# Two blocks of conditioning products moved ahead of the sums of squares, with their landing places, before the first MLP

## The chip, the cores and the metric

The kernel runs on one core of one Trainium2 chip. The metric is the device time of one execution in microseconds (us); several executions are taken and their median is quoted. TensorE (PE in the profile) multiplies, VectorE (DVE) and ScalarE (ACT) work on tiles element by element, GpSimd (POOL) does a few small things, SyncE (SP) issues the DMA transfers. Each engine has its own instruction stream, works it off in order, and waits on semaphores for the others.

## The reference

Two layers over 512 latent and 256 context tokens of width 1024. What matters here is layer 0: a pooling mixer, a gated residual, a root-mean-square norm with a shift and a scale that come from a conditioning vector, and a squared-ReLU MLP.

```
sh1, sc1, g1, sh2, sc2, g2 = split(silu(c) @ ada_w[i] + ada_b[i], 6)     # six vectors of 1024
h = h + g1 * pool_mix(modulate(rms_norm(h, norm_g[i, 0]), sh1, sc1))
m = rms_norm(h, norm_g[i, 1]) * (1 + sc2) + sh2
h = h + g2 * (square(relu(m @ mlp_w1[i])) @ mlp_w2[i])
```

The same is done for the context tokens with a second conditioning vector. The product `silu(c) @ ada_w[0]` has 6144 columns and is cut into twelve blocks of 512: blocks 6 and 7 are the shift `sh2`, blocks 8 and 9 the scale `sc2`, blocks 10 and 11 the second gate.

## The kernel before

Activations lie with the 1024 features on the partitions, as eight tiles of 128 features (`KT` = 8); a tile has 512 latent columns (`h_lat`) and 256 context columns (`h_ctx`).

A block b of the conditioning is made in two steps. `ada0_products(b)` loads four pieces of 512 KB (`adaw[0, b, u]`) and multiplies them on TensorE, eight matmuls of 512 columns that use 32 columns of the array each (L192; a matmul shows as two records); ACT then copies the sums to a row (L195). `ada0_done(b)` transposes that row on TensorE (L201), DVE sums it and adds the bias (L204, L206), and for some blocks makes the factor `am` (L160). Below, P6 is the products of block 6, T6 its transposes, and so on.

Where the pieces land differs by block. Most go into a ring of seven buffers (`praw`), two pieces into a ring called `mc`, blocks 6 and 8 into two large tiles, `m_hi` and `m_lo`, that held the turned inputs of the mixer until its last pooling matmul and will hold the MLP's input afterwards. Block 4 had landed in two buffers of the ring `w`, in which the weights are split into a high and a low part (`load_w`: ACT copies, L91; DVE subtracts, L92).

The loop over `dt` makes the eight output tiles of the mixer (L668); DVE adds each to `h` (L353), ACT squares it, and POOL adds the squares into one tile for latent and one for context (L272, `accs`). The last tile's squares are left in tiles of their own (`tails`, L680). Then come, in this order on TensorE: P6, the sums of squares over the partitions (matmuls against a column of ones, 24 records, L287), T6, P8, the spreading of the reciprocal roots over the partitions (12 records, L302; the roots are made by DVE at L289 and POOL at L291), T8, P9, and the first MLP matmuls.

The MLP's input is made in twelve units, in the order latent, latent, context of two feature tiles each. For unit u, `normed(u)` multiplies on DVE (L737 latent, L735 context), `moved(u)` makes the high part on ACT (L748; for context L745 twice and L746), `used(u)` makes the low part on DVE (L759, L757) and issues the unit's six latent or twelve context matmuls (L764) against the first two weight tiles (`ws`). The loop runs normed(u), moved(u-1), used(u-2); it is written out by hand, and so is the order on TensorE from the mixer on, and on DVE and ACT from the sums of squares to the units' end. Elsewhere a scheduler places instructions. TensorE's products of block 10 (P10) are placed by it between the units.

Of the kernel before, what the change touches and what calls it, by code (L numbers as in the profile page):

```python
# [8 lines left out]
F32 = mybir.dt.float32  # L9
F32R = mybir.dt.float32r  # L10
AF = mybir.ActivationFunctionType
# [3 lines left out]
P = 128  # L15
D = 1024
KT = D // P
# [30 lines left out]
def dit_block_kernel(ctx: ExitStack, tc: tile.TileContext, xT, cols, adab, adaw, w1, w2, wqkv, wo,  # L48
                     poolw, gvec, rope, edge, eye, out):
    nc = tc.nc  # L50
    act, dve, pool, pe = nc.scalar, nc.vector, nc.gpsimd, nc.tensor
# [5 lines left out]
    big = sb(ctx, "big", 1)  # L57
    wp = sb(ctx, "wp", 4)
    rp = sb(ctx, "rp", 2)
    sc = sb(ctx, "sc", 4)  # L60
# [14 lines left out]
    def new(p, shape, dt, tag, bufs=None):  # L75
        uid[0] += 1
        kw = {"bufs": bufs} if bufs else {}
        return p.tile(shape, dt, tag=tag, name=f"{tag}{uid[0]}", **kw)
# [8 lines left out]
    def ps_aux():  # L87
        return new(aux, [P, 512], F32, "aux")
# [21 lines left out]
    landing = {}  # L110
# [35 lines left out]
    def load_w(src, lo_eng=dve, ring=None, raw=None):  # L146

        t = new(wp, [P, 2, 1024], F32R, "w")
        if raw is None:
            raw = new(*(ring or (raws, [P, 1024], F32, "raw")))  # L150
            nc.sync.dma_start(raw, src)
        hilo(t[:, 0], t[:, 1], raw, lo_eng)
        return t
# [19 lines left out]
    def ada0_products(b):  # L173

        ps = ps_aux()
        for u in range(4):
            if (b, u) in ((5, 3), (9, 3)):

                t = new(mc, [P, 1024], F32, "mc")
                nc.sync.dma_start(t, adaw[0, b, u])  # L180
            elif b in landing:
                t = landing[b][:, u]
                nc.sync.dma_start(t, adaw[0, b, u])
            elif early:
                t = early.pop(0)
            else:
                t = new(*praw)
                nc.sync.dma_start(t, adaw[0, b, u])
            for kk in range(2):
                kt = 2 * u + kk  # L190
                o = kt % CG * (P // CG)
                pe.matmul(ps[o : o + P // CG, :512], s_w[:, kt], t[:, kk * 512 : kk * 512 + 512],  # L192
                          start=kt < CG, stop=kt >= KT - CG)
        row = new(sc, [P, 512], F32, "sc")
        act.activation(row, ps[:, :512], AF.Copy)  # L195
        return row
# [48 lines left out]
    def hs(k0, k1, c0, n):  # L245

        if c0 < SEQ:
            return h_lat[:, k0:k1, c0 : c0 + n]
        return h_ctx[:, k0:k1, c0 - SEQ : c0 - SEQ + n]
# [14 lines left out]
    def squares(acc, k, w, c0, n, place=None, eng=dve):  # L264

        if acc is None:
            acc = new(accp[0], [P, w, n], F32, accp[1]) if place is None else place
            act.activation(acc, hs(k, k + w, c0, n), AF.Square)
        else:
            sq = new(sc, [P, w, n], F32, "sc")  # L270
            act.activation(sq, hs(k, k + w, c0, n), AF.Square)
            eng.tensor_tensor(acc, acc, sq, op=ALU.add)  # L272
        return acc
# [386 lines left out]
    accs = [None, None]  # L660
# [7 lines left out]
                pe.matmul(ps[:, c0 : c0 + w], lhs, pooled[dt // 2][:, kc, ax, c0 : c0 + w], start=n == 0, stop=n == 5)  # L668
        return ps

    tails = []

    def mixed(dt, ps):
        for s, c0, n in segs:
            add_gated(dt, ps[:, c0 : c0 + n], gp, c0, n)
            if dt < KT - 1:
                accs[s] = squares(accs[s], dt, 1, c0, n, eng=pool)
            else:
                tails.append(new(sc, [P, 1, n], F32, "sc"))
                act.activation(tails[s], hs(dt, dt + 1, c0, n), AF.Square)  # L680

    row = ada0_products(2)
    tile0 = pool_tile(0)
# [8 lines left out]
    for dt in range(8):  # L692
        ps = mix(dt)
        if dt in (0, 3):
            row = ada0_products(3 + 2 * (dt > 0))
        elif dt == 4:
            ada0_done(5, row)
        mixed(dt, ps)
        if dt == 1:
            ada0_done(3, row)  # L700
        if dt in (1, 2, 3, 4):
            scaled(*pool_tile(dt + 3))

        if dt == 4:
            for b, tag in ((6, "m_hi"), (8, "m_lo")):
                landing[b] = big.tile([P, 4, D], F32, tag=tag, name=f"block{b}")
            ws = [load_w(w1[0, t]) for t in range(2)]
        if dt == 5:
            row = ada0_products(7)
        elif dt == 6:  # L710
            ada0_done(7, row)
    row = ada0_products(6)

    by_hand.enter_context(tc.manual_schedule(engines={mybir.EngineType.DVE, mybir.EngineType.Activation}))
    stats = ps_aux()
    rrs = [rstd_cols(n, [accs[s], tails[s]], stats[:, 4 * s : 4 * s + n // P]) for s, _, n in segs]
    ada0_done(6, row)
    row = ada0_products(8)  # L720
    rbs = [spread(rrs[s], n, ps_aux()[:, :n]) for s, _, n in segs]
    ada0_done(8, row)
    m = new_m("m")

    units = [u for k in range(0, KT, 2) for u in ((0, k, 1), (0, k + 1, 1), (1, k, 2))]
# [41 lines left out]
    for u in range(len(units) + 2):  # L767
        if u < len(units):
            normed(u)
        if 0 < u <= len(units):  # L770
            moved(u - 1)
        if u > 1:
            used(u - 2)

        if u == 1:
            last = ada0_products(9)
        elif u == 3:
            ada0_done(9, last)
    ws = [load_w(w1[0, 2 + t]) for t in range(2)]
    by_hand.close()  # L780
# [439 lines left out]
```

## Time and profile before

| | |
|---|---|
| three runs, median | 1252.46 us (1251.32 to 1253.43) |
| the profiled execution, its own time | 1251.34 us |
| its span, first to last instruction | 1249.2 us |
| mean granted TensorE clock | 0.996 of 2.4 GHz |
| TensorE busy | 1222.6 us, 98% |
| DVE, ACT, POOL busy | 1016.9, 589.5, 143.1 us |

The stretch that the change touches runs from about 25 us (where block 4's buffers come free) to about 96 us (the end of the units). The profile gives each engine's instructions with a start and a duration, and in brackets the idle time before it with what ended it; the granted clock is 1.00 at 2.4 GHz and 0.50 at 1.2 GHz.

### The profile page before, as it was taken

How to read it: one execution, taken by the hardware profiler on the slowest of the kernel's cores; microseconds unless marked ns; L12 is line 12 of the kernel's file. 1: busy time of each engine (PE TensorE's matmuls, PEld its weight loads, DVE VectorE, ACT ScalarE, POOL GpSimd, SP SyncE). 2: the span in 40 equal slices, each digit the busy share in tenths (PEclk: the TensorE clock that was granted, in tenths of full speed). 3: DMA queues.
4: the chain of work that ended last, by engine and by line, in shares of the span. 5: the costliest groups of instructions: out<-in, count | busy, mean ns of one | idle time of the engine just before them, and what ended most of it. 6: DMA issues, size and time to landing. Idle time of an engine off the chain costs nothing.

```text
span 1249.2 us, 20001 instructions
## 1 busy us (share of the span) xinstructions
PE 1222.6 (98%) x7896; PEld 1080.2 (86%) x7896; DVE 1016.9 (81%) x1723; ACT 589.5 (47%) x1055; POOL 143.1 (11%) x129
## 2 busy tenths in 40 slices
PE   7999999999999999999999999999999999999996
PEld 4767888899999999999988888888988999999996
DVE  6564998888989788866888387879899989898986
ACT  6554533444444444334455264554565454545443
POOL 0300000122131322231012001000000000000002
PEclk9999999999999999999999999999999999999998
DMA  9866424333433333321122020211223332323201
GB/s 351 329 238 218 136 85 139 114 119 119 153 111 133 129 123 120 129 68 34 46 82 85 17 85 18 68 34 67 102 86 101 111 109 92 111 94 110 75 28 68
DMA packets 41310, 138.64 MB, mean 111 GB/s; under 512 B 4736, under 2 KB 8064, under 8 KB 41088
## 3 DMA queue, kind: packets, MB, share of 16 engines
q1 hardware_dynamic: 41216, 137.36, 32.0%
q8 instruction: 62, 1.02, 0.3%
q14 instruction: 32, 0.26, 0.1%
HBM read 135.25 MB, written 2.10 MB: 110 GB/s over the span
## 4 chain that ended last, share of the span: by engine, by line
PE 63%; issue 27%; DVE 4%; ACT 2%; DMA 2%; POOL 1%; SPq 0%; POOLq 0%; DVEq 0%; ACTq 0%
PE aux L495 10%; PE mm L495 10%; PE aux L889 7%; PE mm L444 5%; PE aux L464 5%; PE mm L376 5%; PE aux L444 4%; PE aux L1009 3%; PE aux L998 3%; PE mm L967 2%; DMA raw<-in_dram 2%; PE aux L192 1%; PE mm L668 1%; PE mm L764 1%; PE aux L988 1%
## 5 line engine op out<-in xcount | busy, mean ns | idle before, releaser
L495 PE MATMUL aux<-act,w 128*128 128x512 f32 (+1 forms) x1224 | 238.8, 346 | 0.3 <-DVE h_lat L353 0.2
L495 PE MATMUL mm<-act,w 128*128 128x512 f32 (+1 forms) x1224 | 237.2, 345 | 0.9 <-DVE h_lat L353 0.9
L495 PEld LDWEIGHTS mm<-act,w 128*128 128x128 f32 x1224 | 194.9, 189 | 31.6 <-DVE h_lat L353 1.1
L495 PEld LDWEIGHTS aux<-act,w 128*128 128x128 f32 x1224 | 194.7, 189 | 29.6 <-DVE h_lat L353 0.7
L92 DVE TENSOR_TENSOR w<-raw,w 128x1024 fp32r<-128x1024 f32 x106 | 129.3, 1224 | 28.4 <-ACT w L91 28.3
L91 ACT ACTIVATE w<-raw 128x1024 fp32r<-128x1024 f32 x106 | 110.2, 1056 | 77.6 <-PE aux L495 40.7
L353 DVE SCALAR_TENSOR_TENSOR h_lat<-aux,mod,h_lat 128x512 f32<-128x512 f32 (+1 forms) x180 | 122.4, 686 | 16.9 <-PE aux L495 14.2
L433 POOL TENSOR_TENSOR sc<-pair 128x512 f32<-128x512 f32 x55 | 80.0, 1462 | 314.2 <-DMA raw<-in_dram 106.7
L353 DVE SCALAR_TENSOR_TENSOR h_lat<-mm,mod,h_lat 128x512 f32<-128x512 f32 (+1 forms) x140 | 97.7, 700 | 5.5 <-PE mm L495 4.6
L376 PE MATMUL mm<-m_m_hi,w 128*128 128x512 f32 (+1 forms) x320 | 92.9, 352 | 0.2 <-ACT m_m_hi L91 0.2
L889 PE MATMUL aux<-w,a_m_hi 128*128 128x256 f32 (+1 forms) x384 | 86.3, 320 | 0.0
L224 DVE SCALAR_TENSOR_TENSOR mc<-raw,s_f,mc 128x512 f32<-128x512 f32 x112 | 83.7, 765 | 2.1 <-DMA raw<-in_dram 1.3
L444 PE MATMUL mm<-m_m_hi,mc 128*128 128x256 f32 x384 | 69.8, 281 | 0.0
L889 PEld LDWEIGHTS aux<-w,a_m_hi 128*128 128x128 f32 x384 | 63.4, 190 | 5.0
L376 PEld LDWEIGHTS mm<-m_m_hi,w 128*128 128x128 f32 x320 | 56.3, 189 | 10.2 <-ACT r L384 0.8
L464 PE MATMUL aux<-m_c,w 128*128 128x256 f32 x528 | 61.6, 276 | 0.0
L889 PE MATMUL aux<-w,a_m_lo 128*128 128x256 f32 (+1 forms) x192 | 61.2, 319 | 0.0
L464 PEld LDWEIGHTS aux<-m_c,w 128*128 128x128 f32 x528 | 60.8, 188 | 0.0
L444 PEld LDWEIGHTS mm<-m_m_hi,mc 128*128 128x128 f32 x384 | 59.4, 188 | 0.5
L291 POOL TENSOR_TENSOR sm<-sm,neghalf 128x2 f32<-128x2 f32 (+1 forms) x9 | 6.6, 738 | 443.4 <-DVE sm L289 443.4
L376 PE MATMUL mm<-m_m_lo,w 128*128 128x512 f32 (+1 forms) x160 | 56.1, 351 | 0.7 <-DVE m_m_lo L92 0.7
L444 PE MATMUL mm<-m_m_lo,mc 128*128 128x256 f32 x192 | 53.9, 281 | 0.0
(260 smaller groups left out, 2453.9 us busy)
## 6 DMA issues: line engine op xcount, KB each, us to landing
raw<-in_dram SPq DMA_DIRECT2D x155, 512.0 KB, 3.8
praw<-in_dram SPq DMA_DIRECT2D x34, 512.0 KB, 7.7
fin<-in_dram SPq DMA_DIRECT2D x24, 512.0 KB, 4.4
pair<-in_dram SPq DMA_DIRECT2D x22, 512.0 KB, 4.6
block<-in_dram SPq DMA_DIRECT2D x8, 512.0 KB, 7.2
h_lat<-in_dram SPq DMA_DIRECT2D x4, 512.0 KB, 6.3
w<-in_dram SPq DMA_DIRECT2D x4, 512.0 KB, 10.7
out_dram<-fin SPq DMA_DIRECT2D x8, 256.0 KB, 2.5
```

Of the source, the lines that this page charges most:

```text
L91: act.activation(hi, src, AF.Copy)
L92: lo_eng.tensor_tensor(lo, src, hi.bitcast(F32), op=ALU.subtract)
L224: dve.scalar_tensor_tensor(acc[:, s], w, scal, acc[:, s], op0=ALU.mult, op1=ALU.add)
L353: dve.scalar_tensor_tensor(h, ps, gate[:, dt, s : s + 1], h, op0=ALU.mult, op1=ALU.add)
L376: pe.matmul(ps[:, c0 : c0 + cn], lhs, ms(m, ax, k, c0, cn), start=k + wx + ax == 0, stop=k == KT - 1 and wx == 1)
L433: eng.tensor_tensor(t, x, y, op=how)
L444: pe.matmul(places[n], w[:, wx, k * P : k * P + P], inputs[n][ax][:, k], start=k + wx + ax == 0, stop=k == 3 and wx == 1)
L464: pe.matmul(pc[:, t * 256 : t * 256 + 256], ws[k // 4][:, wx, k % 4 * P : k % 4 * P + P], ms(m, ax, k, SEQ, CTX), start=k + wx + ax == 0, ...
L495: pe.matmul(ps, lhs, a[:, t, ax, c0 : c0 + n], start=t + wx + ax == 0, stop=t == 1 and wx == 1)
L889: pe.matmul(ps, lhs, ws[u][:, wx, o : o + width], start=k + ax + wx == 0, stop=k == KT - 1 and ax == 1)
L998: pe.matmul(po, v[:, vx, k, g * HD : g * HD + HD], pT[:, px, k, j0:j1].rearrange("p j q -> p (j q)"), start=k + vx + px == 0, stop=k == 5 ...
L1009: pe.matmul(ps, ws[j][:, wx, dt * P : dt * P + P], o[ax][:, j, c0 : c0 + n], start=j + wx + ax == 0, stop=j == 1 and ax == 1)
```

## The change

Block 7 lands in two buffers of the ring `w` (those that block 4 used); block 6 lands in the `praw` ring; only block 8 keeps a large tile, `m_hi`. The first two weight tiles `ws` are made behind the mixer's loop in the program instead of in its fifth step. P8 stands directly behind P6 and ahead of the sums of squares, T8 directly behind T6. The last tile's squares are added to `accs` by DVE, so that the sums of squares take one tile each and not two. P9 is issued at unit step 2 instead of 1, T9 at step 4 instead of 3.

```diff
         for u in range(4):
-            if (b, u) in ((5, 3), (9, 3)):
+            if b == 7:
+                if u % 2 == 0:
+                    pair = new(wp, [P, 2, 1024], F32, "w")
+                t = pair[:, u % 2]
+                nc.sync.dma_start(t, adaw[0, b, u])
+            elif (b, u) in ((5, 3), (9, 3)):
...
     def mixed(dt, ps):
         for s, c0, n in segs:
             add_gated(dt, ps[:, c0 : c0 + n], gp, c0, n)
-            if dt < KT - 1:
-                accs[s] = squares(accs[s], dt, 1, c0, n, eng=pool)
-            else:
-                tails.append(new(sc, [P, 1, n], F32, "sc"))
-                act.activation(tails[s], hs(dt, dt + 1, c0, n), AF.Square)
+            accs[s] = squares(accs[s], dt, 1, c0, n, eng=pool if dt < KT - 1 else dve)
...
         if dt == 4:
-            for b, tag in ((6, "m_hi"), (8, "m_lo")):
-                landing[b] = big.tile([P, 4, D], F32, tag=tag, name=f"block{b}")
-            ws = [load_w(w1[0, t]) for t in range(2)]
+            landing[8] = big.tile([P, 4, D], F32, tag="m_hi", name="block8")
...
-    row = ada0_products(6)
+    ws = [load_w(w1[0, t]) for t in range(2)]
+    rows = [ada0_products(6)]
...
+    rows.append(ada0_products(8))
     stats = ps_aux()
-    rrs = [rstd_cols(n, [accs[s], tails[s]], stats[:, 4 * s : 4 * s + n // P]) for s, _, n in segs]
-    ada0_done(6, row)
-    row = ada0_products(8)
+    rrs = [rstd_cols(n, [accs[s]], stats[:, 4 * s : 4 * s + n // P]) for s, _, n in segs]
+    ada0_done(6, rows[0])
+    ada0_done(8, rows[1])
     rbs = [spread(rrs[s], n, ps_aux()[:, :n]) for s, _, n in segs]
-    ada0_done(8, row)
...
-        if u == 1:
+        if u == 2:
             last = ada0_products(9)
-        elif u == 3:
+        elif u == 4:
             ada0_done(9, last)
```

TensorE, from the last product of block 6 to the first unit. `aux_` tiles are banks of PSUM, `sc_` the rows and squares, `mc_425` and `mc_428` the summed squares, `sm_` the roots. Before (line 192 is a product, 287 the sums of squares, 201 transposes, 302 the spreading, 764 a unit):

```order
L287 MATMUL aux_714<-ones,sc_695 128x1
L201 MATMUL aux_735<-ident,sc_710 128x128 x4
L192 MATMUL aux_743<-block_598,s_w_146 32x512 x8
L302 MATMUL aux_758<-ident,sm_725 128x128 x4
L302 MATMUL aux_763<-ident,sm_733 128x128 x2
L201 MATMUL aux_766<-ident,sc_756 128x128 x4
L192 MATMUL aux_788<-praw_789,s_w_146 32x512 x2
```

Of the change, the same place (198 a product, 293 the sums of squares, 207 transposes, 308 the spreading, 763 a unit):

```order
L198 MATMUL aux_717<-block_597,s_w_146 32x512 x8
L293 MATMUL aux_732<-ones,mc_425 128x1 x4
L293 MATMUL aux_732<-ones,mc_428 128x1 x2
L207 MATMUL aux_747<-ident,sc_713 128x128 x4
L207 MATMUL aux_755<-ident,sc_730 128x128 x4
L308 MATMUL aux_764<-ident,sm_739 128x128 x4
L308 MATMUL aux_769<-ident,sm_745 128x128 x2
L763 MATMUL mm_778<-m_m_hi,w_686 128x512
```

P8 has moved ahead of the sums of squares, whose matmuls are half as many; behind them stand both transposes, the spreading, and then a unit.

ACT, from the row of block 8 to the first context unit (`aux_743` and `aux_788` are the products of blocks 8 and 9). Before:

```order
L195 ACTIVATE sc_756<-aux_743 128x512
L748 ACTIVATE m_m_hi<-sc_783,mod_132 128x512
L195 ACTIVATE sc_805<-aux_788 128x512
L748 ACTIVATE m_m_hi<-sc_785,mod_132 128x512
L745 ACTIVATE sc_807<-sc_807,mod_132,am_136 128x256 x2
L746 ACTIVATE m_c_777<-sc_807 128x512
```

Of the change (`aux_717` and `aux_795` are the products of blocks 8 and 9):

```order
L201 ACTIVATE sc_730<-aux_717 128x512
L747 ACTIVATE m_m_hi<-sc_780,mod_132 128x512
L747 ACTIVATE m_m_hi<-sc_782,mod_132 128x512
L201 ACTIVATE sc_812<-aux_795 128x512
L744 ACTIVATE sc_785<-sc_785,mod_132,am_136 128x256 x2
L745 ACTIVATE m_c_774<-sc_785 128x512
```

The copy of block 9's row stood between the high parts of units 0 and 1; it stands now directly ahead of the first context unit.

DVE, around the sum of block 9's transposes (`aux_829` before, `aux_842` in the change). Before:

```order
L759 SCALAR_TENSOR_TENSOR m_m_lo<-sc_785,mod_132,m_m_hi 128x512
L204 TENSOR_REDUCE sm_834<-aux_829 128x8
L206 TENSOR_TENSOR mod_132<-sm_834,bcol 128x8
L160 SCALAR_TENSOR_TENSOR am_136<-mod_132,pcol 128x8
L737 SCALAR_TENSOR_TENSOR sc_838<-h_lat,am_136,aux_758 128x512
L757 TENSOR_TENSOR m_c_779<-sc_807,m_c_777 128x512
```

Of the change:

```order
L736 SCALAR_TENSOR_TENSOR sc_826<-h_lat,am_136,aux_764 128x512
L756 TENSOR_TENSOR m_c_776<-sc_785,m_c_774 128x512
L210 TENSOR_REDUCE sm_847<-aux_842 128x8
L212 TENSOR_TENSOR mod_132<-sm_847,bcol 128x8
L160 SCALAR_TENSOR_TENSOR am_136<-mod_132,pcol 128x8
L734 TENSOR_TENSOR sc_851<-h_ctx,aux_769 128x512
L758 SCALAR_TENSOR_TENSOR m_m_lo<-sc_814,mod_132,m_m_hi 128x512
```

The wait for block 9's transposes stood ahead of the low part of unit 2; it stands now behind it, ahead of the low part of unit 3.

## Rows read from the trace of the kernel before

**Rows 1.** The page, busy time of the engines over the span.

```profile
PE 1222.6 (98%) x7896; PEld 1080.2 (86%) x7896; DVE 1016.9 (81%) x1723; ACT 589.5 (47%) x1055; POOL 143.1 (11%) x129
```

**Rows 2.** Waits of TensorE from 95 to 300 us: us in total, times, longest.

```profile
PE aux L791 <- DVE s_w L786: 0.5, 1, 0.5
PE aux L796 <- ACT sc L793: 0.5, 1, 0.5
```

**Rows 3.** The chain of waits from 50 to 100 us: start, us on the chain, what.

```profile
60.91 1.85 PE aux L192 x16
62.76 1.89 PE aux L287 x16
64.67 0.17 DVE sm L289
...
64.98 1.02 PE aux L287 x8
66.01 0.50 PE aux L201 x4
66.50 2.81 PE aux L192 x16
69.31 2.21 PE aux L302 x12
71.52 0.45 PE aux L201 x4
...
75.47 2.88 PE mm L764 x11
...
94.81 0.98 PE aux L192 x4
```

**Rows 4.** Busy time in three stretches (us from the span's start; the number behind POOL's is the granted clock, then the DMA engines' share and GB/s).

```profile
66.00:67.00 1.00, 1.00 (x13) 0.54 (x15) 0.52 (x3) 0.00 (x0) 0.70 (x1) 1.00 1.05 422
67.00:68.00 1.00, 1.00 (x12) 0.23 (x7) 0.00 (x0) 0.00 (x0) 0.00 (x0) 0.63 1.01 401
68.00:70.00 2.00, 2.00 (x11) 0.76 (x4) 0.00 (x0) 0.58 (x1) 0.00 (x0) 0.50 1.02 408
```

**Rows 5.** Timeline of DVE in the first units: start, us, instruction, idle before it and what ended that.

```profile
72.75 1.41 DVE L737 SCALAR_TENSOR_TENSOR sc<-h_lat,am,aux 128x512 f32<-128x512 f32 x2
...
78.83 0.19 DVE L204 TENSOR_REDUCE sm<-aux 128x8 f32<-128x32 f32 x1 [1.96 <-PE aux L201]
...
79.33 0.74 DVE L737 SCALAR_TENSOR_TENSOR sc<-h_lat,am,aux 128x512 f32<-128x512 f32 x1
79.99 0.68 DVE L757 TENSOR_TENSOR m_c<-sc,m_c 128x512 fp32r<-128x512 f32 x1
80.60 0.68 DVE L735 TENSOR_TENSOR sc<-h_ctx,aux 128x512 f32<-128x512 f32 x1
81.19 0.74 DVE L759 SCALAR_TENSOR_TENSOR m_m_lo<-sc,mod,m_m_hi 128x512 fp32r<-128x512 f32 x1
```

**Rows 6.** Timeline of ACT, rows of blocks 6 and 9 and the first units.

```profile
62.89 0.60 ACT L195 ACTIVATE sc<-aux 128x512 f32<-128x512 f32 x1 [0.16 <-PE aux L192]
...
74.17 0.58 ACT L195 ACTIVATE sc<-aux 128x512 f32<-128x512 f32 x1
74.64 0.71 ACT L748 ACTIVATE m_m_hi<-sc,mod 128x512 fp32r<-128x512 f32 x1
75.26 1.08 ACT L745 ACTIVATE sc<-sc,mod,am 128x256 f32<-128x256 f32 x2
76.37 0.63 ACT L746 ACTIVATE m_c<-sc 128x512 fp32r<-128x512 f32 x1
```

**Rows 7.** Timeline of TensorE around block 9's transposes and units 2 and 3.

```profile
78.19 0.60 PE L201 MATMUL aux<-ident,sc 128*128 128x128 f32 x4
...
78.84 1.91 PE L192 MATMUL aux<-praw,s_w 128*32 128x512 f32 x12
80.73 1.56 PE L764 MATMUL mm<-m_c,w 128*128 128x256 f32 x11
82.13 0.39 PE L764 MATMUL mm<-m_m_hi,w 128*128 128x512 f32 x1
82.36 0.39 PE L764 MATMUL mm<-m_m_lo,w 128*128 128x512 f32 x1
```

**Rows 8.** The squares and the weight split: timeline rows of ACT, POOL and DVE, and the durations of DVE's own additions of squares elsewhere in the kernel (least, median, most in ns).

```profile
61.79 0.63 ACT L680 ACTIVATE sc<-h_lat 128x512 f32<-128x512 f32 x1 [1.60 <-DVE h_lat L353]
60.02 1.98 POOL L272 TENSOR_TENSOR mc<-mc,sc 128x512 f32<-128x512 f32 x2 [2.19 <-ACT sc L271]
64.92 1.02 POOL L291 TENSOR_TENSOR sm<-sm,neghalf 128x4 f32<-128x4 f32 x1 [2.91 <-DVE sm L289]
43.29 2.50 POOL L272 TENSOR_TENSOR mc<-mc,sc 128x512 f32<-128x512 f32 x2 [2.38 <-ACT sc L271]
42.73 1.22 DVE L92 TENSOR_TENSOR w<-raw,w 128x1024 fp32r<-128x1024 f32 x1
L272 DVE TENSOR_TENSOR mc<-mc,sc x9: 681/685/692, 605.6 to 900.5; 128x512 f32<-128x512 f32 x9
```

**Rows 9.** The transfers of blocks 6 and 8: their issue on SP's queue (start, us), and the time from issue to landing.

```profile
51.73 3.83 SPq L183 DMA_DIRECT2D block<-in_dram  x8
...
DMA to landing us min/median/max: 3.6/7.2/10.3
```

More of the change, by code (lines that the diff above doesn't have):

```diff
@@ L669, in mix @@
         return ps
-    tails = []
     def mixed(dt, ps):
```

## The prediction

> **What bounds the kernel now.** I read the busy times first: TensorE is busy 98% of the span [rows 1]. So a change of this size can gain only where TensorE waits, runs at the lower clock, or does work that can be dropped. Next, who makes TensorE wait behind the stage: from 95 to 300 us it waits 0.5 us twice and no more [rows 2], so time saved by about 96 us should reach the end, and time lost too. Then the chain of waits through the stage [rows 3]. P6 ends at 62.76 and the first `normed` starts at 72.75 [rows 5]. These 10 us are a serial path: sums of squares of the latent columns 1.89, the hand-over to DVE and back 0.33 (64.65 to 64.98), those of the context 1.02, T6 0.50, P8 2.81, spreading 2.21, T8 0.45, and small steps of DVE. Two of them are dearer than their kind: P6, the same work as P8, took 1.85, and transposes of the spreading's shape (T8) took 0.45 for four, 0.11 each, against 0.18 in the spreading. The stretches of busy time say why: the granted clock is 1.00 to 67 us, 0.63 in the next and 0.50 from 68 to 70 [rows 4], that is 1.2 GHz, after some 3 us of one-column matmuls. Behind 72.75 the units are a second path: DVE waits 1.96 us for T9 [rows 5], and TensorE fills the time with P10 until unit 2's low part is there at 80.73 [rows 7].
>
> **The change part by part.** I follow the path from the end of P6, 62.76. What lies ahead of it keeps its length, because TensorE has P3, P5, P7, P6 and the mixer in the same order and was busy throughout.
>
> *P8 ahead of the sums.* 62.76 + 1.85 (P6's price, full clock) = 64.61. This hides the longer making of the squares: ACT squares at 61.79 for 0.63; DVE's own addition of 128x512 takes 0.69 elsewhere [rows 8], so latent sums are whole at about 63.2 and the context's by 63.9 (a second addition at no more than 0.69). Without P8 as cover it would cost about 0.4 us. The two weight splits that the order on DVE now puts at the mixer's sixth and seventh tile take 1.22 each [rows 8]; they may be slowed by POOL's additions, or slow these: two of POOL's took 2.50 beside such a split and 1.98 alone [rows 8]. Such 0.5 us twice would bring the latent sums to 64.2, still ahead of 64.61. ACT's half of the splits falls into its idle time ahead of each tile's squares, 1.60 us before the last [rows 8]. All this I put at nothing; at worst, with both delays and the context sums last, 0.5.
>
> *The landings.* Block 8 was last of eight transfers issued from 51.73 on, the slowest of which landed after 10.3 us [rows 9], that is up to 65.4, too late for a P8 at 62.76. It is now first of its group, four of 512 KB; block 6 takes the buffers of block 3, which are free long before; block 7 earlier than before. Nothing is due late. Cost nothing; if block 8 still landed as the last did, P8 would wait up to 2.6.
>
> *Half the sums.* One tile and not two: 0.95 to 65.56, hand-over 0.33 to 65.89 (the bank is still shared), context 0.51 to 66.40, T6 0.50 to 66.90, T8 0.45 to 67.35. The roots are not late: POOL ended at 65.94 before, 1.3 behind the latent sums [rows 8], so now at 66.9. Spreading of the latent columns, eight records at 0.11, 0.90 to 68.25 (at 0.18 each, its own price at the lower clock, 1.47). T8's tail on DVE (71.97 to 72.75 before) ends at 68.13 and hides. `normed(0)` starts at 68.30, 4.45 us earlier than before.
>
> *P9 and T9 one unit later.* Here most of it is given back. Unit 0's low-part matmul comes 2.72 behind `normed(0)` (75.47 against 72.75): 71.02. Its five matmuls at 0.26 (eleven in 2.88 [rows 3]) end at 72.33, and only then P9, 1.85, to 74.18. ACT's copy of its row now stands ahead of the first context unit, and everything of that unit stands behind it. The copy starts 0.13 behind the products (62.89 against 62.76), the next on ACT 0.47 later, the context steps take 1.74 (75.26 to 77.00) [rows 6]: 76.52. DVE's low part 0.68 and 0.06 to TensorE (79.99 to 80.73) [rows 5, 7]: 77.26. TensorE has done unit 1 (six matmuls at 0.26) by 75.8 and waits 1.5. Unit 2 to the next start takes 1.40 (80.73 to 82.13): 78.66, where T9 now stands, 0.60, and DVE takes it up at 79.30 (0.04, as at 78.83). It is 0.50 to the next `normed` (78.83 to 79.33), 0.59 to the low part (80.60 to 81.19), 0.74 for it, 0.06 to TensorE: unit 3's low-part matmul at 81.19, against 82.36 before [rows 5, 7]. Of 4.45 us 1.17 are left.
>
> *P10.* Before, six of its eight matmuls ran in the wait ahead of unit 2 (twelve records, 1.91 [rows 7]) and two at 94.81 for 0.98 [rows 3]. Now the order has five in the wait behind T9 (1.6 at that rate, hidden), then one alone, then two. The two cost 0.98 again. One alone is not in the trace: between 0.23 (an eighth of 1.85) and 0.98. Four records cost 0.98 where sixteen cost 1.85, so the price is not by record; I take 0.90. T10 and P11 only change places with other TensorE work. What is left is 1.17 - 0.90 = 0.3 us, with the bounds of this term 0.2 to 0.9.
>
> The profiled execution took 1251.34 us, and would take 1251.0. It lies 1.1 under the median of the three runs, 1252.46, within their 2.1 us of spread; from the median the sum gives 1252.2, which is my forecast. About 0.2%, 2.5 us, is what a measurement of this kernel can tell from no change.
>
> **A rule against it.** The lower clock came at 67 us after sparse matmuls, and the array was still at 1.2 GHz up to 70 [rows 3, 4]. The change moves P8 out from between the sums and the spreading, so that from 64.6 to 71.0 TensorE has small matmuls and a wait. The Trainium skill (TensorE: Matmul & The Clock Gate, "What's actually happening") has it that the throttled clock is the default state and activity releases it; by that rule the fall could come again, later, on work that is now on the path. By the rows alone the sum has no such term, since 128-column transposes with gaps kept 1.00 at 66 to 67; by the rule it would be the first rival's.
>
> **The rivals.**
> *The clock falls at unit 0.* Place: the wait for unit 0's low part. Unit 0's five matmuls cost 1.31 more and P9 0.96 more (2.81 against 1.85): 1252.2 + 2.3 = 1254.5. If it falls already in the spreading and lasts through P9, 0.57 more, 1255.1: slower by over 0.2% from the point where the fall outlasts P9. For it: the sparse stretch above. Against it: only half as many one-column matmuls are left, and transposes and spreading fill the middle of that stretch. Chance 0.22, of which 0.08 past the bound.
> *The front's gain stays.* If block 9's row does not hold up ACT, the wait of 1.5 ahead of unit 2 goes: 1250.7; if T9's wait goes too, 4.45 - 0.90 are kept: 1248.9. For it: the front is the plainest part of the sum. Against it: the order has copy and context unit on one in-order engine. Chance 0.10, of which 0.06 past the bound.
> *The first MLP gives something away.* The scheduler's order behind the units changes with the start; DVE now makes an addition of 128x1024 for the Strassen inputs ahead of the product that the rest of the shift waits for. At 1.22, the price of such an operation [rows 8]: 1253.4 to 1253.7. Against it: two short waits in 200 us leave room. Chance 0.10.
> *The forecast*, between 1251 and 1253.2 with the unknown prices and the runs' spread: 0.58.
>
> **How the numbers follow.** The range leaves out the far end of the second rival and the far end of the first: 1249.8 to 1254.8. Faster by over 0.2%: 0.06 from the second rival and 0.02 for luck of the runs, 0.08; slower 0.08 from the first and 0.02, 0.10; the same 0.82.
>
> **What would show it.** In the profile after: P8 right behind P6 in about 1.85 us; twelve records in the sums of squares; `normed(0)` near 68.3; ACT idle ahead of the copy of block 9's row and the first context unit near 74.8 to 76.5; TensorE's unit 2 near 77.3 and unit 3's low part near 81.2; a granted clock of 1.00 from 66 to 76. Wrong would be the forecast if unit 3 starts before 80 (the copy did not hold ACT), if the clock shows 0.50 at unit 0, or if new waits of TensorE appear past 96 us.

## The result and the profile after

The changed kernel takes 1252.55 us (median; 1251.75 to 1255.18), the kernel before, run beside it on the same chip, 1251.3. The ratio is 1.0014 with an interval of 1.0007 to 1.002: slower by 0.14%, where 0.02% faster was forecast. The time lies inside the range; the side was wrong. The profiled execution took 1253.05 us (span 1251.0), against 1251.34 (span 1249.2) of the one before.

The chain of waits of the changed kernel (start, us on the chain, what; 198 a product, 293 the sums, 207 transposes, 308 the spreading, 736 a latent `normed`, 201 the copy of a row, 744 and 745 the context unit on ACT, 756 its low part, 763 a unit) answers to [rows 3]:

```profile
64.50 1.00 PE aux L293 x8
...
65.74 0.61 PE aux L293 x4
66.34 0.93 PE aux L207 x8
67.28 0.91 PE aux L308 x8
...
68.21 0.47 DVE sc L736
...
70.93 2.50 PE mm L763 x5
73.43 2.34 PE aux L198 x16
...
75.85 0.60 ACT sc L201
76.45 0.99 ACT sc L744 x2
...
78.12 0.70 DVE m_c L756
...
78.86 1.52 PE mm L763 x11
80.39 0.44 PE aux L207 x4
...
84.48 0.97 PE aux L198 x2
...
86.92 0.98 PE aux L198 x4
```

Down to 70.93 this is the forecast to 0.1 us: `normed(0)` at 68.21 (68.30), the first low part on TensorE at 70.93 (71.02). Then unit 0's five matmuls take 2.50 and not 1.31, P9 2.34 and not 1.85. From there the chain goes over ACT's copy of block 9's row and the context unit, as forecast, 1.6 us late; unit 3's low part comes at 82.82 (81.19), and the broken P10 costs 0.97 and 0.98. TensorE in stretches (busy, records, granted clock, DMA share, GB/s) says why the two were long; it answers to [rows 4]:

```profile
66.00:70.00 4.00, 2.85 (x25) 1.00 1.02 410
70.00:71.00 1.00, 0.34 (x2) 0.91 1.04 414
71.00:74.00 3.00, 3.00 (x9) 0.50 0.16 63
74.00:75.00 1.00, 1.00 (x12) 0.89 0.00 0
```

The fall that stood at 67.3 to 70.7 us in the kernel before is gone, and another stands at 70.8 to 74.2, on the path: the place of the first rival. The experiments and the other executions show that it is a small part of the loss.

Two measures are used for all kernels. The **front** ends with the start of `normed(0)`. The **length** runs from there to the first matmul behind the units (line 376 before, 382 after: a high part against the next weights). T10 and P11 are counted in: where they stand behind that matmul, their 2.38 us (100.04 to 102.42 in the kernel before) are added. In the first profiles: before 72.75 and 25.35 (95.72 - 72.75 + 2.38), after 68.21 and 31.75 (to 99.96).

### The profile page after: what moved, and what is told of

It is laid out like the page before. It is cut to its first block, busy times and chain, and to the rows that moved or that the text cites. A ratio compares the mean times of both kernels' runs of the same rounds, so it can differ in the third digit from the quotient of the medians.

```text
span 1251.0 us, 19981 instructions
## 1 busy us (share of the span) xinstructions
PE 1222.9 (98%) x7884; PEld 1078.7 (86%) x7884; DVE 1021.5 (82%) x1725; ACT 588.3 (47%) x1055; POOL 142.8 (11%) x129
## 4 chain that ended last, share of the span: by engine, by line
PE 65%; issue 27%; DVE 3%; ACT 2%; POOL 1%; DMA 1%; SPq 0%; POOLq 0%; DVEq 0%; ACTq 0%
PE mm L501 10%; PE aux L501 10%; PE aux L888 7%; PE mm L382 6%; PE mm L450 5%; PE aux L470 5%; PE aux L450 4%; PE aux L1008 3%; PE aux L997 3%; PE aux L198 2%; PE mm L966 2%; PE mm L674 1%; PE mm L763 1%; PE aux L987 1%; PE mm L967 1%
```

## Experiments: block 9 put back, and moved alone

**Back at step 1.** The changed kernel with one part undone.

```
-        if u == 2:
+        if u == 1:
             last = ada0_products(9)
-        elif u == 4:
+        elif u == 3:
             ada0_done(9, last)
```

> The changed kernel with one part undone: the products of block 9 stand again at unit step 1 (ahead of unit 0's matmuls) and its transposes at step 3, as in the kernel before; all else is the change. My theory: the whole loss of the change comes from the later place of block 9, in two ways: the granted clock falls to 0.50 from about 70.9 to 74.1 us, on unit 0's five matmuls (2.50 instead of 1.31 us) and on P9 (2.34 instead of 1.85), and ACT's copy of block 9's row holds the context unit. With P9 back, its 1.85 us fill the wait from 68.6 to 70.9, the clock stays at 1.00 or its fall is hidden, the copy stands between two latent high parts, and unit 2's low part comes 7.98 us behind normed(0), as before (72.75 to 80.73): near 76.2. The 4.5 us of the front stay: 1246.5 to 1248, ratio to before 0.996 to 0.9975. Rival (the front's gain would be lost to DVE or POOL in the units or later, whatever the place of block 9): 1251 to 1253, the ratio within 0.2% of 1.

Measured: 1247.08 us (1246.92 to 1248.09), ratio 0.9962 (0.9949 to 0.9974), faster than both kernels. Front 68.52, length 25.68. Timeline of TensorE behind the spreading:

```profile
68.85 1.48 PE L198 MATMUL aux<-praw,s_w 128*32 128x512 f32 x10
...
70.71 0.50 PE L763 MATMUL mm<-m_m_hi,w 128*128 128x512 f32 x1
71.23 0.50 PE L763 MATMUL mm<-m_m_lo,w 128*128 128x512 f32 x1
...
76.81 1.56 PE L763 MATMUL mm<-m_c,w 128*128 128x256 f32 x11 [0.83 <-DVE m_c L756]
```

P9 fills the wait ahead of unit 0, the granted clock is 1.00 through the whole stage, and the front's gain stays. The rival (DVE or POOL takes the gain whatever block 9's place) falls.

**Late in the kernel before.** The same four lines changed the other way in the kernel before, nothing else.

> The kernel before with one part of the change alone: the products of block 9 at unit step 2 instead of 1, its transposes at step 4 instead of 3. My theory (late block 9 costs what the front gives): unit 3's low part 3.3 us later than before by the order alone (81.19 + 4.45 against 82.36), one product of block 10 standing alone 0.9 to 1.0, together 4.2: 1255.5, ratio 1.0034; if the low clock is on unit 0 and P9 here too, 1.7 more: 1257.2, ratio 1.0047. Rival (the later place is nearly free, and the loss comes from the other parts): within 0.2% of before.

Measured: 1256.68 us, ratio 1.0038 (1.0025 to 1.005). Front 71.49 (no fall of the clock ahead of it here), length 31.93, with the clock at 0.50 from 75.3 to 78.7, on unit 0 and P9. So the later place costs 5.2 to 5.5 us in either kernel, 1256.68 against 1251.44 and 1252.55 against 1247.08, and the rest of the change saves 4.1 to 4.4.

## Experiments: the clock

**Filler.** Matmuls that no result uses, in the two waits around unit 0's first matmul.

```
+    def filler(k):
+        for i in range(k):
+            o = i % CG * (P // CG)
+            pe.matmul(stats[o : o + P // CG, 128:512], s_w[:, i], h_lat[:, 7, :384], start=True, stop=True)
+    filler(6)
...
+                        if k + wx + ax == 0 and s == 0 and wt is ws[0]:
+                            filler(3)
```

> The changed kernel with work added that no result uses: nine matmuls of 32x384 into a spare part of the bank of the sums, six between the spreading and unit 0's first matmul and three between that and its low part, where TensorE waits 1.15 and 0.66 us. Nothing else moves. Theory 1 (the granted clock fell in these waits, and its fall costs 1.7 us on unit 0 and P9): the clock stays at 1.00 from 70 to 76 us, unit 0's five matmuls take about 1.3 and P9 1.85, unit 3's low part comes near 81.2, and the time is 1.5 to 1.7 us under the changed kernel: about 1250.9, 0.9995 of before. Theory 2 (the fall is settled earlier, by the sums and the transposes from 64.5 us on): the clock falls all the same, and the time is that of the changed kernel, 1.001 of before. Theory 3 (unit 0 and P9 are slow for another reason than the clock, for instance what else is running then): the clock is 1.00 and the two still take 2.5 and 2.3.

Measured: 1252.98 us, ratio 1.001 (1.000 to 1.002): the time of the changed kernel. In its profile the clock is 1.00 from 60 to 1243 us, unit 0 and P9 take 1.36 and 1.85, and the length is 30.55. One such profile shows little, since two of four profiles of the unaltered kernel keep the clock too (below). The mean granted clock of each execution says more: it is 0.997 or 0.998 in all ten executions with filler that enter the ratio, and 0.996 in nine of 33 without. So the filler most likely keeps the clock up, as in theory 1, but the sum of theory 1 does not hold: that was not worth 1.6 us in the median, which is the time of executions that keep the clock anyway. The filler has a price of its own, too: unit 0's low part comes 2.96 us behind `normed(0)` (71.59 and 68.63), and 2.72 without it.

**The same kernel again.** The changed kernel, unaltered, three times more, and the kernel before twice.

> The changed kernel itself, unaltered, profiled a second time. In its first profile the granted clock fell to 0.50 from 70.9 to 74.1 us, on unit 0 and P9; in the kernel with block 9 at step 3 TensorE had the same waits ahead of unit 0 (1.15 and 0.66 us) and the clock stayed at 1.00; and with filler in these waits it stayed too, yet the time was 1252.98. Theory 1 (the fall belongs to this order and comes in every execution): 0.50 again at unit 0, unit 3's low part near 82.8, span near 1251. Theory 2 (it comes in some executions and not in others): in this profile the clock may stay at 1.00, then unit 0's five matmuls take 1.3 and P9 1.85, unit 3's low part comes near 81.2, the span is up to 1.7 shorter, and the times of the runs lie up to 1.7 us apart; the median stays 1252 to 1253.

> A third profile of the changed kernel. With a fall of the clock at unit 0 and P9 (as in its first profile): unit 3's low part near 82.8, 1253.0; without (as in its second): near 81.5, 1251.8. The products of the last block before the first layer's second product (eight records pairs at 121.0 us, 2.84 and 2.95 us so far where 1.92 is their price) wait for a landing in both: again 2.7 to 3.0.

> A fourth profile of the changed kernel, with the same two cases as the third: 1253.0 with a fall of the clock at unit 0, 1251.8 without. If a time is far from both (1254 or more), the place where it was lost is past 96 us, and not in the stage.

> The kernel before itself, profiled a second time. The sum of the prediction was made against one profiled execution (1251.34 us), in which the granted clock fell to 0.50 from 67.4 to 70.7 us. Theory (falls of the clock in this stage come in some executions and not in others, and the profiled one was a dear one): without a fall P8 takes 1.85 and not 2.81, the spreading of eight latent and four context records 1.5 and not 2.21, so normed(0) comes 1.6 to 1.8 earlier, near 71.1, and the execution takes 1249.2 to 1249.8; with a fall it is like the first, 1251.0 to 1251.6. Rival (the fall is in every execution of before): 0.50 at 67 to 70 us again, and the times of before differ for another reason, to be seen past 96 us.

> A third profile of the kernel before, with the same two cases: with a fall of the clock near 67 us 1251.0 to 1251.6 and normed(0) near 72.7, without one 1249.2 to 1249.8 and normed(0) near 71.1. Between 208 and 303 us the changed kernel and all experiments lost 0.4 us against the first profile of before; if that belongs to the first profile alone, these two show the later marks 0.4 us later too, measured from the end of the units.

Measured: the profiled executions of the changed kernel took 1251.76 and 1252.73 us with the clock at 1.00 through the stage, and 1254.37 with 0.50 from 72 to 75.4 us; those of the kernel before 1253.16 and 1251.49 us, both with a fall. With the first of these, eleven executions of the changed kernel have a median of 1252.7 us, ratio 1.001 (1.0002 to 1.0019). The first row is the second profile of the changed kernel, the next the fourth; the last two are the kernel before, second and third:

```profile
71.00:74.00 3.00, 2.86 (x21) 1.00 0.25 101
```

```profile
72.00:75.00 3.00, 3.00 (x15) 0.50 0.05 19
```

```profile
66.00:72.00 6.00, 6.00 (x27) 0.50 1.03 411
```

```profile
67.00:69.00 2.00, 2.00 (x13) 0.50 1.04 418
```

One program, the same waits, and the clock falls in two profiles of four; in the kernel before in three of three, for 3.4 to 6.8 us, with the front at 72.75, 74.48 and 73.11. The expectation that before could go without a fall was met by none of its profiles (the front of 71.49 above is what it would be), but by other executions of it. The mean granted clock is on record for each execution. In all 17 profiles the clock is below 1.00 only between 65 and 79 us and in the last microseconds; the four with a mean of 0.998 have no fall in the stage, the six with 0.996 or less have one, and 0.997 comes with and without.

| executions, by mean clock | number | us | median |
|---|---|---|---|
| before, beside the second profile of the change: 0.998 | 9 of 34 | 1249.02 to 1250.56 | 1249.54 |
| the same: 0.994 | 6 of 34 | 1252.99 to 1255.01 | 1253.14 |
| after, the 22 of the first section: 0.998 | 10 of 22 | 1251.75 to 1252.72 | 1252.38 |
| the same: 0.996 | 7 of 22 | 1253.05 to 1255.18 | 1254.18 |

So the fall comes in about a third of the executions of the changed kernel, and its median, 1252.55, is close to that of executions without one. The profiles side by side (us; the end is the start of the last sums of squares, near 1240):

| | front | length | from there to the end |
|---|---|---|---|
| before, three profiles | 72.75, 74.48, 73.11 | 25.35, 25.33, 25.35 | 1142.13, 1142.25, 1142.45 |
| after, clock kept | 68.42, 68.43 | 30.28, 30.29 | 1142.51, 1143.02 |
| after, clock fell | 68.21, 68.47 | 31.75, 31.92 | 1142.51, 1143.31 |

Means: front -5.06, length +4.94 and the fall +0.78 (1.55 in two of four), the rest +0.56: +1.22 us. That this is the loss of the medians (1.25) is partly luck, since the fall hardly enters the median of the changed kernel. The median of the kernel before, 1251.3, most likely has one: its first profile, with a fall of 3.4 us, took 1251.34. Against that profile the two of the changed kernel that kept the clock give -4.32 for the front, +4.93 for the length and +0.64 for the rest: +1.25 with no fall of its own. Without a fall in either kernel the change loses more, 2.7 us by the executions at 0.998 on one chip (1252.24 in six of the second profile's eleven, against 1249.54): 1.26 us of the front's gain are the fall that the change takes away there (72.75 against 71.49).

The 0.4 us between 208 and 303 us, of which the expectation for the third profile of before speaks, belong in part to its first profile alone: from the small matmuls of line 240 (246 after) near 208 us to those near 310 its three profiles take 101.20, 101.45 and 101.45 us, the four of the changed kernel 101.59 to 101.60.

## Experiments: which wait the later place makes

**Block 9 one step later still** (products at step 3, transposes at step 5).

> The changed kernel with the products of block 9 one step later still (step 3, behind unit 1's matmuls) and its transposes at step 5, the last that is in time for unit 6. ACT's copy of its row then stands behind the first context unit's steps and not ahead of them. Theory (the copy on ACT's in-order stream is what holds the context unit, and P9 behind unit 0 is not wrong in itself): ACT makes the context unit from about 70.4 on, unit 2's low part is ready near 74, and TensorE has matmuls without a wait from unit 0 to unit 3, whose low part comes near 78, or near 79.5 with unit 0 at the low clock. From there the products of block 10 (1.85 here, none hidden) count. Sum: units 18.6 + P9 1.85 + T9 0.5 + P10 1.85 from 70.93 end at 93.7 against 95.7 before: 1249.3, or 1251 with the low clock: ratio 0.9984 to 0.9998, and 1.6 to 3.3 us under the changed kernel. Rival (the transposes of block 9 and DVE's sums behind them set the units' pace, wherever the copy is): as late as the changed kernel or later, 1252.5 to 1254.

Measured: 1249.21 us, ratio 0.998 (0.997 to 0.999); length 26.96. As the theory has it: with the copy behind the context unit nothing holds ACT, and the rival (1252.5 to 1254) falls.

**The copy alone, the transposes alone, both.** For the first, the copy is split from the products and issued at the end of step 3; for the second `elif u == 4` becomes 5; for the third both.

```
         if u == 2:
-            last = ada0_products(9)
+            last = ada0_products(9, copied=False)
+        elif u == 3:
+            last = ada0_row(last)
         elif u == 4:
             ada0_done(9, last)
```

> The changed kernel with one thing moved: ACT's copy of block 9's row stands behind the first context unit's steps (end of unit step 3) and not ahead of them; products at step 2 and transposes at step 4 as in the change. It prices the hold on ACT alone. Measure: from the start of normed(0) to the first matmul behind the units (with T10 and P11 done): 25.34 us in three profiles of before, 30.28 in those of the changed kernel without a fall of the clock, 31.8 with one. Theory: the context steps run from 70.4 on, DVE's low part is ready near 73.8, and unit 2's low part comes as soon as TensorE is through P9 and unit 1, 7.9 us behind normed(0) instead of 9.16: 1.3 earlier; T9 as much earlier; and three products of block 10 at the end in one piece instead of two pieces, 1.1: length 27.9, time 1250.2 without a fall, 1251.7 with one. Rival (the transposes of block 9 alone set the pace, the copy only fills the time until they can come): unit 3's low part still 13.1 behind normed(0), and only the 1.1 of block 10: 1251.5 to 1252.7.

> The changed kernel with one thing moved: block 9's transposes at step 5 and not 4; products at step 2, ACT's copy ahead of the context unit as in the change. It prices the wait of DVE for the transposes alone (2.05 us in the changed kernel's profile). Theory: unit 2's low part stays 9.2 behind normed(0), but unit 3's comes right behind unit 2, 10.9 behind normed(0) and not 13.15; the products of block 10 are then paid in one piece (1.85 and 0.11) where five of them stood in the wait and three cost 2.17 in pieces: length 28.0 instead of 30.28, time 1250.3 without a fall of the clock, 1251.8 with one. Rival (the copy on ACT alone sets the pace; DVE's wait for the transposes is hidden under TensorE's work): 1252 to 1253.

> Both of the other two: ACT's copy behind the context unit and block 9's transposes at step 5, the products at step 2 as in the change. Theory: TensorE has no wait left behind unit 0's low part, so that the two savings (2.3 and 2.4) do not add: length 26.9 to 27.1, as with the products at step 3 (26.96), time 1249.2 without a fall of the clock, 1250.7 with one. Rival (they add): 25.6, as with the products back at step 1, 1247.2 to 1248.

Measured: copy alone 1248.88 us (ratio 0.9976; 0.9968 to 0.9985), length 27.27; transposes alone 1251.72 (1.0001; 0.9992 to 1.001), length 28.03; both 1249.88 (0.9989; 0.9979 to 0.9998), length 26.35. TensorE of the first, then of the second, around unit 2's low part and T9 (their idle time and what ended it in brackets):

```profile
75.32 0.39 PE L766 MATMUL mm<-m_m_hi,w 128*128 128x512 f32 x1
75.55 1.58 PE L766 MATMUL mm<-m_c,w 128*128 128x256 f32 x12
76.97 0.60 PE L210 MATMUL aux<-ident,sc 128*128 128x128 f32 x4
```

```profile
76.79 0.38 PE L763 MATMUL mm<-m_c,w 128*128 128x256 f32 x1 [0.86 <-ACT m_c L745]
77.51 1.56 PE L763 MATMUL mm<-m_c,w 128*128 128x256 f32 x11 [0.34 <-DVE m_c L756]
78.91 0.40 PE L763 MATMUL mm<-m_m_hi,w 128*128 128x512 f32 x1
```

In the first the waits ahead of unit 2 are gone; in the second they stay, and unit 3 follows unit 2 at once. Of the 4.9 us that the later place costs in length, the hold on ACT is worth 3.0 and DVE's wait for T9 2.25; together they give 3.9 and not 5.25, since TensorE then has no wait left behind unit 0's low part. The expectations were met in part. For the copy the rival falls (1251.5 to 1252.7), and the gain is larger than the theory's. For the transposes the length is that of the theory, 28.0, but the median of 1251.72 lies between theory (1250.3) and rival (1252): the profiled execution, 1250.10, was the shortest of the eleven. For both, the length lies between the theory (26.9) and adding up (25.6). In the first, unit 2's low part comes about 1.6 us earlier behind `normed(0)`, and three products of block 10 stand in one piece (0.99) where the changed kernel has 0.97 and 0.98; in the second, P10 is paid whole.

**T9 at step 5 with P9 at step 1.** The aim is to beat the fastest version so far.

> The kernel with block 9's products back at step 1 (1247.08 us), with its transposes at step 5 and not 3, the last place that is in time for unit 6. Theory (behind unit 1 DVE waits 1.97 us for the transposes, and unit 2's low part for DVE; TensorE is idle 0.83 us there, with half of block 10's products as filling): DVE goes on to unit 2 at once, its low part comes near 74.6 and not 76.81, TensorE has no wait in units 0 to 3, and the products of block 10 are paid in full: 0.5 to 0.8 us under 1247.1, 1246.3 to 1246.6, ratio to before about 0.9957. Rival (the wait moves to unit 4 or 6, where DVE then waits for the transposes, and TensorE idles there): 1247 to 1248.

Measured: 1248.34 us, ratio 0.9977: 1.26 over the version with T9 at step 3. The length is 24.99, 0.69 shorter as the theory said, so the wait did not move to unit 4 or 6 as the rival had it. What was gained went elsewhere, into the products of block 1: they take 3.63 us (114.72 to 118.35) and not 2.04, and the product behind them starts at 121.88 where it started at 121.72. The rest of the 1.26 was not followed. TensorE there, with T9 at step 3 and then at step 5:

```profile
115.64 2.04 PE L198 MATMUL aux<-praw,s_w 128*32 128x512 f32 x16
```

```profile
114.72 1.91 PE L198 MATMUL aux<-praw,s_w 128*32 128x512 f32 x12
117.30 1.05 PE L198 MATMUL aux<-praw,s_w 128*32 128x512 f32 x4 [0.67 <-DMA praw<-in_dram]
```

The last piece of block 1 lands too late. The same product took 2.22 us in the kernel before and 2.84 in the changed one, and in the version with both moves (copy and transposes) it waits 1.97:

```profile
119.55 2.22 PE L192 MATMUL aux<-praw,s_w 128*32 128x512 f32 x16
```

```profile
121.03 2.84 PE L198 MATMUL aux<-praw,s_w 128*32 128x512 f32 x16
```

```profile
119.94 1.05 PE L198 MATMUL aux<-praw,s_w 128*32 128x512 f32 x4 [1.97 <-DMA praw<-in_dram]
```

SP's queue, before and after, shows what stands ahead of that transfer, which goes out at 116.86 and 118.36:

```profile
113.97 0.33 SPq L215 DMA_DIRECT2D raw<-in_dram  x1
116.86 0.33 SPq L188 DMA_DIRECT2D praw<-in_dram  x1
```

```profile
112.10 6.07 SPq L221 DMA_DIRECT2D raw<-in_dram  x2
118.36 0.33 SPq L194 DMA_DIRECT2D praw<-in_dram  x1
```

In both it goes out 1.09 us behind the start of P0 (115.77 and 117.27), when a buffer comes free; before, the last 512 KB ahead of it had gone out 3 us earlier, after, just ahead of it, and it lands in 4.4 us and not 3.8. All kernels in which T10 and P11 come ahead of the first matmul behind the units have a dear P1 (2.65 to 4.9 us), all others a cheap one (2.0 to 2.35). Why the scheduler's order of the loads follows the place of P11 was not tried.

In the changed kernel itself the dear P1 is made good at once. P0 comes 0.26 us earlier behind the end of the length (17.40 in the mean of four profiles, 17.66 of before's three), and before, TensorE waited 0.5 to 0.8 us for DVE at the next products. These start 27.73 us behind the end of the length after, 27.72 before; in the first profiles:

```profile
125.85 1.07 PE L791 MATMUL aux<-pw,s_w 128*32 128x256 f32 x16 [0.50 <-DVE s_w L786]
```

```profile
127.39 1.07 PE L790 MATMUL aux<-pw,s_w 128*32 128x256 f32 x16
```

## Experiments: the parts of the front

Both are edits of the version with block 9 back at step 1 (1247.08 us), so that no late copy hides them.

**The last squares in tiles of their own**, as before (24 one-column records, not 12).

```
+    tails = []
...
-            accs[s] = squares(accs[s], dt, 1, c0, n, eng=pool if dt < KT - 1 else dve)
+            if dt < KT - 1:
+                accs[s] = squares(accs[s], dt, 1, c0, n, eng=pool)
+            else:
+                tails.append(new(sc, [P, 1, n], F32, "sc"))
+                act.activation(tails[s], hs(dt, dt + 1, c0, n), AF.Square)
...
-    rrs = [rstd_cols(n, [accs[s]], ...
+    rrs = [rstd_cols(n, [accs[s], tails[s]], ...
```

> The kernel with block 9's products back at step 1 (1247.08 us), with the sums of squares as in the kernel before: the last tile's squares stay in tiles of their own, and 24 records of one column add them, not 12. It prices the half sums. By the rows: 0.95 for the latent and 0.51 for the context sums more, 1.46 together: normed(0) near 70.0 and 1248.5 us. Rival 1 (with 24 one-column records the clock falls behind them, as before at 67 us): the spreading and P9 at 1.2 GHz, 0.6 and up to 1 us more, 1249 to 1250. Rival 2 (DVE's two additions, 1.03 us each here, ended only as the sums began, so that half of the saving was eaten by them): 1247.6 to 1248.

Measured: 1250.12 us, 3.0 more. The front is 70.48, 1.96 later, and the clock is at 0.50 from 68.8 to 72.3: the spreading takes 2.58 where it took 1.50, and P9 in the wait behind it no longer fits.

```profile
68.66 2.58 PE L308 MATMUL aux<-ident,sm 128*128 128x128 f32 x12
```

This is rival 1, with a time just past its range. The one execution of eleven at a mean clock of 0.998 took 1248.31 us, near the 1248.5 of the sums alone.

**P8 back between the sums and the spreading.**

```
-    rows.append(ada0_products(8))
     stats = ps_aux()
...
     ada0_done(6, rows[0])
+    rows.append(ada0_products(8))
```

> The kernel with block 9's products back at step 1 (1247.08 us), with block 8's products again behind the transposes of block 6, between the sums and the spreading; half sums, landings and all else as in the change. It prices P8's place. Theory: the squares are whole at about 64.3 (latent) and 64.8 (context), DVE's two additions being the last; without P8 as cover the sums wait for them from 62.9 on, and P8's 1.85 stand on the path behind: normed(0) 1.4 to 1.9 later, 1248.5 to 1249.0 us. Rival 1 (P8 hid nothing but its own length, and the squares are early enough): 1.85 later at once, with no wait ahead of the sums. Rival 2 (the clock falls again between sums and spreading, as in the kernel before): P8 near 2.8, the spreading at 0.18 a record, 2.8 to 3.3 later, 1250 to 1250.5.

Measured: 1251.04 us, 4.0 more, and 1249.14 to 1254.34 from run to run; the profiled run took 1253.59. TensorE:

```profile
64.65 1.03 PE L293 MATMUL aux<-ones,mc 128*128 128x1 f32 x8 [1.50 <-DVE mc L278]
...
67.84 3.64 PE L198 MATMUL aux<-block,s_w 128*32 128x512 f32 x16
...
73.17 2.75 PE L308 MATMUL aux<-ident,sm 128*128 128x128 f32 x12
```

Without P8 as cover the sums wait 1.50 us for DVE's additions, as the theory said; then the clock is 0.50 from 65.5 to 75.8 us, and P8 costs twice its price. That is more than either theory had for an execution with a fall. Without one the theory comes near: five of the twelve executions have a mean clock of 0.998 and took 1249.14 to 1249.44 us, 2.1 to 2.4 more than 1247.08, and four have 0.994, as the profiled one, and took 1253.10 to 1254.34. By the rows the two parts were worth 1.46 and 1.4 to 1.9; their medians gave 3.0 and 4.0, and in both profiles a large part of the difference stands where the clock is low.

## Why the prediction was wrong

- **The front** was right: `normed(0)` at 68.2 to 68.5 in four profiles (forecast 68.30), P8 behind P6 without a wait for its landing, twelve records of sums, T8's tail hidden. DVE's additions were late, as feared, and hidden: they ended as the sums began. The sum had the profile of before with the shortest front to compare with; over its three profiles the gain is 5.06 and not 4.45.
- **P9 and T9 one unit later** was right in mechanism and nearly in size: unit 3's low part 13.15 us behind `normed(0)` in the third profile, with the clock kept (81.58 and 68.43), where the steps gave 12.89. That is a loss of 3.54 and not 3.28. The two waits were both real, as the split of the copy and of T9 showed, but the hold on ACT was worth 3.0 and not the 1.5 of the wait that the prediction saw ahead of unit 2: P10's place hangs on it too.
- **P10 was mis-sized**: from unit 3's low part to the end of the length 17.14 us in that profile (to 98.72), before 15.74 (82.36 to 98.10): 1.40 and not 0.90. The lone matmul cost 0.97; about 0.3 more is that the first matmul behind each of three pieces takes some 0.1 longer (0.34 and not 0.23 at 82.82 to 83.16 and at 85.38 to 85.72, in the first profile).
- **What lies past the units, put at nothing, failed.** The prediction had time saved by 96 us reach the end, and T10 and P11 "only change places with other TensorE work". From the end of the length on, the changed kernel takes 0.56 us more. With T10 and P11 the loads change places too, and P1 waits for its last piece: 2.84 to 3.34 us in the four profiles, 2.04 to 2.22 in the three of before. But that is made good by the next products, as shown above. The 0.56 comes up behind them: from their start to the small matmuls of line 240 (246 after) near 276 us before takes 150.52 to 150.60 us in its three profiles, after 150.96 to 151.31 in four, with no wait of TensorE that before does not have. Its cause stays open. In every kernel with T10 and P11 ahead this stretch takes 150.96 us or more, but with block 9 back at step 1, where they stand as before, it takes 151.17 too. The third rival named this stretch, with twice the size; the wait for DVE that it feared does not show here.
- **The clock term, put at nothing, failed too**, though the median loses without it. The sum took the fall of before as gone for good ("128-column transposes with gaps kept 1.00"). It came again, at unit 0 and P9, for 1.55 us, in two of four profiles and, by the mean clock, in seven of 22 executions. The first rival had the place, and with 1254.5 the time of those seven (median 1254.18); its chance of 0.22 was a little low. The Trainium skill (TensorE: Matmul & The Clock Gate, "What's actually happening") notes of the rise of the clock at a kernel's start that its moment varies from run to run; here the fall varies too, in four profiles of one program.
- **That 1252.2 is close to 1252.55 is luck.** The three executions that the forecast started from have a median of 1252.46, 1.16 above that of all 22 of the kernel before (1251.3). This hid that the change itself was forecast with the wrong sign.

In one line: forecast -4.45 + 3.28 + 0.90 = -0.3; measured -5.06 + 4.94 (3.54 and 1.40) + 0.78 + 0.56 = +1.2 in the mean of the profiles, and -4.32 + 4.93 + 0.64 = +1.25 from the first profile of before to executions of the change that keep the clock.

## What to carry to other kernels

Work moved out of a gap leaves the gap behind: P9 had filled a wait of TensorE and let its copy slip between two short steps of ACT, and with it there all five executions have a mean clock of 0.997 or 0.998. Put back there, the rest of the change is worth 0.4%. When a stage's clock falls in some executions and not in others, one profile is no base for a sum of tenths of a us: take several, sort the executions by their mean clock, and enter the fall with its share of them, in both kernels. And follow each moved product to the loads that its buffers release, as far as the next one that lands late.

## What the runs showed of the hardware

- Matmuls of 32 columns of the array cost by groups of four here: one (two records) 0.97 us, two 0.98, three 0.99, four 1.00, eight (a whole block) 1.85, on the chain of waits of the changed kernel and of those with the copy behind and with block 9 back at step 1. The Trainium skill (TensorE: Matmul & The Clock Gate, "Part 3: Packing small matmuls — row/col tiling") says that matmuls at different column positions run concurrently; the rows agree, and a matmul broken off alone costs nearly as much as four.
- A 128x8 addition of DVE (the bias of block 7) took 1.25 us beside POOL's addition of squares (60.04 to 62.62 us), and 0.17 otherwise:

```profile
60.71 1.25 DVE L212 TENSOR_TENSOR mod<-sm,bcol 128x8 f32<-128x8 f32 x1
```

```profile
67.17 0.17 DVE L212 TENSOR_TENSOR mod<-sm,bcol 128x8 f32<-128x8 f32 x1
```

The last tile's addition to `h` came about 0.9 us later (61.88, before 60.95), hidden under P6 and P8. No experiment took POOL's addition away, so POOL as the cause is argued and not shown.
